# Hybrid attention block on one core: output banks by which branch ended first, and early merges in front of a step's low parts

## Chip, core and metric

One core of a Trainium2 chip runs the whole program. The time is device microseconds of one execution, and lower is better. The engines are TensorE (PE, with its weight loads as PEld), VectorE (DVE), ScalarE (ACT), GpSimd (POOL) and SyncE (SP), which here only issues transfers.

## The reference, cut to what matters

The block normalises a sequence of 1024 tokens, projects it once, and runs two groups of attention heads on the result: a native sparse attention with 8 query heads in 2 groups, and a latent attention with 8 heads. Both are gated, joined, projected back and normalised. The change touches the sparse attention alone. Each of its query tiles of 128 tokens is attended three times:

```python
s_cmp = einsum('bsghd,bngd->bghsn', qg, kc) * scale        # compressed keys (63 of them)
o_cmp = einsum('bghsn,bngd->bsghd', softmax(s_cmp), vc)
s     = einsum('bgqhd,bgqnkd->bgqhnk', qc, kg) * scale     # selected blocks of 64 keys, causal
o_slc = ...                                                # (top 16 of 16 blocks: all causal keys)
s_win = einsum('bnqghd,bnkgd->bnghqk', qw, kband) * scale  # window of 512 keys
o_win = ...
o = g[..., 0:1] * o_cmp + g[..., 1:2] * o_slc + g[..., 2:3] * o_win
```

## The kernel before

**Units, branches, blocks, pairs.** The sparse attention goes over 16 units `u`: query tile `t = u // 2` and head group `g = u % 2`, four heads side by side in 512 columns. A unit has three branches: 1 the window, 2 the compressed keys, 0 the selected blocks. A branch is cut into blocks of 128 keys; the compressed branch is a single block. The list `blocks` names them in order: for each unit the window's blocks with the compressed block put in after the second of them (before the only one of tile 0), and then the selected blocks. Two neighbours of the list make a pair, 74 in all, and pair `i` may end one unit and begin the next. Unit 0 and unit 1 have 3 blocks each, units 2 and 3 have 5, units 4 and 5 have 7.

**A step.** The loop at the end of the listing runs step `i` over the pairs. `scores(i)` are four matmuls and up to two mask matmuls into one of three score buffers in PSUM. `exps(i)` are two exponentials on ACT, one to f32 (`E`) and one to f16 (`H`). `lows(i - 1)` is one DVE subtraction (`L` = `E` - `H`, line 1010). Then come the merges of what ended in the step before, and `weigh(i - 3)`, the 24 small matmuls by which the pair's weights meet the values (line 937). At a branch's last block, `weigh` returns the branch, and the next step merges it: `merge` (lines 953 to 970) takes a reciprocal of the row sums, multiplies by the gate, and scales the 128 x 256 outputs into the tile `mixn` (line 964, the first branch of a unit) or into `tmp` (line 967), which POOL adds to `mixn` (line 968).

**Banks.** The outputs of a branch are summed in one of two PSUM banks, `o0` and `o1`. The window's lie in bank 1, those of the two other branches in bank 0. A bank's next user waits on the chip until the merge of the last one has read it. PE's instructions are in the order in which the program is written, while those of the other engines are put in order ahead of time by a scheduler that takes what is ready, earlier lines first.

**Staging a unit.** `prep(u)` (lines 850 to 860) readies a unit's queries. Two transfers copy 64 rows into `qa`, PE transposes 24 columns of negative row maxima into an output bank (`nmT`, line 855), DVE copies them out (`mr`, line 857), and four transfers put them over the first six rows of the unit's own query tile (line 859). The first score matmul of a block reads `qa` (line 994), the second reads the tile with the new rows (line 995). Units 0 to 3 are staged earlier. `prep_next(u + 3)`, called in each step behind `weigh`, stages the next unit of `todo` when it is no more than three ahead, and only if no window branch is under way in bank 1.

**Side work.** From step 4 on, each step also does one piece of the list `work`: weights of the latent attention are loaded through one buffer named `raw`, and split by ACT and DVE into high and low parts (lines 1050, 1051, 1062, and 1080 for the four loads `wq`). Masks are made by POOL and cast by DVE (line 870).

Of the kernel before, what the change touches and what calls it, by code (L numbers as in the profile page):

```python
# [53 lines left out]
EARLY = 2  # L54
# [6 lines left out]
CMP_AT = (1, 12, 20, 28, 30, 44, 52, 60)  # L61
LAG = 3
SIDE = 4
SIDE_LAT = 36
LATE = 44
E_MIX = 8
# [28 lines left out]
def f32(ap):  # L95
    return ap.bitcast(F32)
# [11 lines left out]
def hybrid_block(ctx, tc, x, c, positions, ada_w, ada_b, norm_g, w_in, cmp_pos, cmp_k_w1, cmp_k_w2,  # L108
# [8 lines left out]
    def pool(stack, name, side="left"):  # L117
        return stack.enter_context(tc.tile_pool(name=name, bufs=1, side=side, reuse_waits="tile"))
# [20 lines left out]
    def o_bank(name, i):  # L139
        return ps_o.tile([P, 512], F32, tag=f"o{i}", name=name, bufs=1)  # L140
# [637 lines left out]
    bm = pool(nsa_s, "bm")  # L778
# [72 lines left out]
    def prep(u, pl, bufs, pn):  # L851
        qa = pl.tile([P, 512], F32R, name=f"qa{u}", tag="qa", bufs=bufs)
        nc.sync.dma_start(f32(qa[:64]), f32(qc[u][:64]))
        nc.sync.dma_start(f32(qa[64:]), f32(qc[u][:64]))
        nc.tensor.transpose(pn[:24, :P], f32(hl24[:, u]), ident)
        mr = pl.tile([24, P], F32, name="mr", tag="mr", bufs=bufs // 2)
        nc.vector.tensor_copy(mr, pn[:24, :P])
        for h in range(4):
            nc.sync.dma_start(f32(qc[u][:6, h * P:(h + 1) * P]), mr[h:24:4])
        staged[u] = qa  # L860
# [74 lines left out]
    def pv(po, c0, ph, pl, n, qs, v, start, stop):  # L935
        for j, (a, lo, hi) in enumerate(((ph, 0, 65), (ph, 65, 129), (pl, 0, 65))):
            nc.tensor.matmul(po[:, c0:c0 + hi - lo], a[:n, qs], v[:, lo:hi], start=start and j == 0, stop=stop and j == 2,  # L937
                             skip_group_check=True)
# [8 lines left out]
    nc.gpsimd.affine_select(emask, emask, pattern=[[-1, P]], compare_op=ALU.is_gt, fill=FAR, base=0, channel_multiplier=1)  # L947
    emr = npool.tile([P, P], F32R, name="emr")
    nc.vector.tensor_copy(emr, emask)
    outs, begun = {}, set()  # L950

    def merge(u, br):
        t, g = divmod(u, G)
        ov = outs.pop(br)[:, :260].rearrange("p (h d) -> p h d", h=4)
        cf = npool.tile([P, 4], F32, name="cf", tag="cf", bufs=4)
        nc.vector.reciprocal(cf, ov[:, :, DH])
        nc.vector.tensor_tensor(cf, cf, gv[:, br, t, g * 4:(g + 1) * 4], op=ALU.mult)
        o, cfb = ov[:, :, :DH], cf[:, :, None].to_broadcast([P, 4, DH])
        if t not in mixes:
            mixes[t] = npool.tile([P, 512], F32, name=f"mixn{t}", tag="mixn", bufs=2)  # L960
        mv = mixes[t][:, g * 256:(g + 1) * 256].rearrange("p (h d) -> p h d", h=4)
        if u not in begun:
            begun.add(u)
            nc.vector.tensor_tensor(mv, o, cfb, op=ALU.mult)  # L964
            return
        tmp = npool.tile([P, 4, DH], F32, name="tmp", tag="tmp", bufs=2)
        nc.vector.tensor_tensor(tmp, o, cfb, op=ALU.mult)  # L967
        nc.gpsimd.tensor_tensor(mv, mv, tmp, op=ALU.add)  # L968
        if br == 0 and g == G - 1:
            nc.sync.dma_start(mix_dram[t * P:(t + 1) * P, :], mixes.pop(t))  # L970

    blocks = []
    for u in range(NT * G):
        t = u // G
        win = [(u, 1, j, j == max(0, t - WIN_T), j == t) for j in range(max(0, t - WIN_T), t + 1)]
        win[min(2, t):min(2, t)] = [(u, 2, 0, True, True)]
        blocks += win + [(u, 0, j, j == 0, j == t) for j in range(t + 1)]
    pairs = [blocks[i:i + 2] for i in range(0, len(blocks), 2)]

    kb_late = npool.tile([P, 2, G, S - KB_CUT * P], F32R, name="kb_late")  # L980

# [4 lines left out]
    def scores(i):  # L986
        pS = ps[0].tile([P, 1024], F32, tag="s", name=f"s{i}", bufs=3)
        for n, (u, br, j, _, _) in enumerate(pairs[i]):
            t, g = divmod(u, G)
            ks = slice(j * P, (j + 1) * P)  # L990
            a, b = (kac[:, g], kbc[:, g]) if br == 2 else (ka[br][g][:, ks], kb_of(j)[:, br, g])
            dst = pS[:, n * 512:(n + 1) * 512]
            mk = cmr[t] if br == 2 else dmr if j == t else emr if br == 1 and j == t - WIN_T else None
            nc.tensor.matmul(dst, a, staged[u], start=True, stop=False)  # L994
            nc.tensor.matmul(dst, b, qc[u], start=False, stop=mk is None)  # L995
            if mk is not None:
                nc.tensor.matmul(dst.rearrange("k (h q) -> k h q", h=4), identr, mk[:, None, :].to_broadcast([P, 4, P]),
                                 start=False, stop=True)
        return pS

    def exps(i, pS):
        Et = npool.tile([P, 1024], F32, name=f"E{i}", tag="E", bufs=EB)
        ph = hlp.tile([P, 1024], F16, name=f"H{i}", tag="H", bufs=HB)
        nc.scalar.activation(Et, pS, AF.Exp, scale=SC_NSA)  # L1004
        nc.scalar.activation(ph, pS, AF.Exp, scale=SC_NSA)  # L1005
        return Et, ph

    def lows(i, Et, ph):
        pl = hlp.tile([P, 1024], F16, name=f"L{i}", tag="L", bufs=HB)
        nc.vector.tensor_tensor(pl, Et, ph, op=ALU.subtract)  # L1010
        return ph, pl

    def weigh(i, ph, pl):
        done = []
        for n, (u, br, j, first, last) in enumerate(pairs[i]):
            g = u % G
            if first:
                outs[br] = o_bank(f"o{u}_{br}", 1 if br == 1 else 0)
            v = vc16[:, g] if br == 2 else v16[:, j, br, g]
            for h in range(4):  # L1020
                pv(outs[br], h * 65, ph, pl, P, slice(n * 512 + h * P, n * 512 + (h + 1) * P), v, first and h == 0, last)
            if last:
                done.append((u, br))
        return done

    next_psum("ps_b")
    todo = list(range(2 * EARLY, NT * G))

    def prep_next(u):
        if todo and todo[0] <= u and 1 not in outs:  # L1030
            prep(todo[0], bm, 2 * EARLY, o_bank(f"nmT{todo[0]}", 1))
            todo.pop(0)

    for u in range(2 * EARLY, 4):
        prep_next(u)
# [86 lines left out]
    def first_part(a):  # L1122
        if a == 0:
            khs.append(key_place("kh1", 0, 0))
        else:
            qhs.append(key_place("qh1", 1, 0))
        kq_second(2 * a)
# [16 lines left out]
    def const_rows(i, tiles, hi):  # L1144
        nc.sync.dma_start(f32(tiles[i][64:hi]), f32(tiles[0][64:hi]))
# [65 lines left out]
    def q_rot_rows(heads, parts=(0, 1)):  # L1211
        for a in parts:
            for h in heads:
                i = h % 4
                nc.sync.dma_start(f32((qhs, qls)[a][h % NSETS][64:96]), f32(qrs[i * 32:(i + 1) * 32, a]))
# [182 lines left out]
    last = [lambda: first_part(0), lambda: const_rows(1, khs, 98), lambda: first_part(1), lambda: q_rot_rows((1,), (0,))]  # L1398
    last2 = peak_leads(1) + [lambda: (peak_split(1), max_rows(1))]
    n_pairs = len(pairs)  # L1400
    s_of, e_of, p_of, m_of = {}, {}, {}, {}
    flow = []
    with tc.manual_schedule(engines={mybir.EngineType.PE}):
        for i in range(n_pairs + LAG + 2):
            if i < n_pairs:
                s_of[i] = scores(i)
                e_of[i] = exps(i, s_of.pop(i))
            if 0 <= i - 1 < n_pairs:
                p_of[i - 1] = lows(i - 1, *e_of.pop(i - 1))
            if n_pairs <= i < n_pairs + LAG:  # L1410
                flow.append((i - n_pairs, *scores_m(i - n_pairs)))
            for u, br in m_of.pop(i - 1, ()):
                merge(u, br)
            if 0 <= i - LAG < n_pairs:
                m_of[i] = weigh(i - LAG, *p_of.pop(i - LAG))
            if i < n_pairs:
                u = pairs[i][-1][0]
                before = len(todo)
                prep_next(u + 3)
                if u % G == 0 and u // G + 1 < NT and u // G + 1 not in cmr:  # L1420
                    next_mask(u // G + 1)
                if i in KB_AT:
                    keys_b(kb_late, KB_CUT * P, S, KB_AT.index(i))
                if i >= SIDE and work:
                    work.pop(0)()
                elif i >= SIDE_LAT and side:
                    if (i - SIDE_LAT) % 2 == 0:
                        side.pop(0)()
                elif i >= LATE and late and (len(late) > 6 or (i - LATE) % 2):
                    late.pop(0)()  # L1430
            if i == LAST_AT:
                for f in last:
                    f()
            if i >= PEAK1 and last2:
                last2.pop(0)()
# [160 lines left out]
```

## Time and profile before

| what | value |
|---|---|
| median of 3 runs | 792.07 us |
| lowest and highest of them | 790.29 and 792.58 us |
| the profiled execution, own time | 788.64 us |
| its span, first to last instruction | 786.9 us |
| PE / DVE / ACT / POOL busy | 94% / 74% / 50% / 29% of the span |
| mean granted clock of TensorE | 0.97 of full speed |

The profiled execution is 3.43 us faster than the median of the runs and 1.74 us longer than its span. The sparse attention lies between 353 and 541 us of the span. Rows of the timeline give the start in us, the duration in us, engine, line, operation, what is written and what it is computed from; brackets at the end hold the idle time just before and the instruction that ended it. Matmuls overlap, so the distance from one start to the next is what a matmul costs.

### The profile page before, as it was taken

Reading aid. Unit: us, or ns where it says so; the run is one execution under the profiler, and the core shown is the slowest. Engines: PE = TensorE matmul, PEld = TensorE weight load, DVE = VectorE, ACT = ScalarE, POOL = GpSimd, SP = SyncE. Lnnn points to the kernel's source line nnn. Section 1 sums busy time; section 2 is a strip of 40 time slices with the busy share of each in tenths; the row PEclk is TensorE's granted clock in tenths of the full one; section 3 lists DMA queues with packets and bytes.
Section 4 is the critical chain, followed back from the end, with each engine's and each line's share of the span. In section 5 each row is a group of like instructions: output and inputs, shape, how many; then the busy total and the mean of one; then the engine's idle time right before and its main releaser. Section 6 shows DMA issues by size and latency. Waiting matters only on the chain.

```text
span 786.9 us, 17257 instructions
## 1 busy us (share of the span) xinstructions
PE 739.3 (94%) x6464; PEld 653.9 (83%) x6464; DVE 583.6 (74%) x1549; ACT 396.3 (50%) x697; POOL 228.0 (29%) x287
## 2 busy tenths in 40 slices
PE   4999999999999999997899999999988989999996
PEld 3988998989999999995677887777877777888885
DVE  3688745587688788888898889987888878654433
ACT  5354534133122331217899977987556566632212
POOL 3334433154231143504443312110200040154322
PEclk9599999999999999999999999999999979999999
DMA  8961423242531121103311123013010140435431
GB/s 307 262 197 49 127 55 108 61 121 80 162 95 48 44 52 47 36 31 97 93 47 44 43 56 82 22 57 80 10 28 16 52 151 29 151 131 185 144 113 54
DMA packets 60513, 70.18 MB, mean 89 GB/s; under 512 B 5957, under 2 KB 46728, under 8 KB 60430
## 3 DMA queue, kind: packets, MB, share of 16 engines
q1 hardware_dynamic: 55646, 64.62, 27.8%
q10 hardware_dynamic: 4784, 4.47, 1.7%
q8 instruction: 51, 0.84, 0.4%
q14 instruction: 32, 0.26, 0.1%
HBM read 48.33 MB, written 11.53 MB: 76 GB/s over the span
## 4 chain that ended last, share of the span: by engine, by line
PE 76%; DVE 9%; issue 4%; ACT 4%; DMA 4%; POOL 2%; SPq 1%; POOLq 0%; DVEq 0%; ACTq 0%
PE pj L589 24%; PE out L1528 11%; PE o L937 5%; PE pm L841 4%; PE s L994 3%; PE s L995 3%; PE kcT L321 2%; PE mo L937 2%; PE hid L642 2%; PE kq L1180 2%; PE ms L1301 2%; DVE L L1010 2%; PE ms L1302 2%; PE ms L1303 2%; PE mm L1256 2%
## 5 line engine op out<-in xcount | busy, mean ns | idle before, releaser
L589 PE MATMUL pj<-whi,hh 128*128 128x288 f32 (+2 forms) x544 | 161.4, 297 | 0.0
L589 PE MATMUL pj<-wlo,hh 128*128 128x288 f32 (+2 forms) x544 | 158.6, 292 | 0.0
L589 PE MATMUL pj<-whi,hl 128*128 128x288 f32 (+2 forms) x544 | 157.6, 290 | 0.0
L589 PEld LDWEIGHTS pj<-wlo,hh 128*128 128x128 f32 x544 | 102.5, 189 | 1.4
L589 PEld LDWEIGHTS pj<-whi,hh 128*128 128x128 f32 x544 | 102.5, 189 | 0.4
L589 PEld LDWEIGHTS pj<-whi,hl 128*128 128x128 f32 x544 | 102.2, 188 | 0.0
L1010 DVE TENSOR_TENSOR L<-E,H 128x1024 f16<-128x1024 f32 x74 | 92.0, 1243 | 13.1 <-ACT H L1005 11.4
L799 DVE CUSTOM_DVE_ANT_0 junk<-pm,maskw 128x256 bf16<-128x256 f32 (+3 forms) x160 | 77.7, 486 | 16.4 <-PE pm L841 4.4
L1004 ACT ACTIVATE E<-s 128x1024 f32<-128x1024 f32 x74 | 76.4, 1032 | 19.8 <-PE s L995 12.2
L937 PEld LDWEIGHTS <-H 128*128 128x128 f16 x1184 | 57.2, 97 | 30.2 <-issue 17.5
L968 POOL TENSOR_TENSOR mixn<-mixn,tmp 128x256 f32<-128x256 f32 x32 | 44.8, 1400 | 108.7 <-DVE tmp L967 101.9
L1005 ACT ACTIVATE H<-s 128x1024 f16<-128x1024 f32 x74 | 76.2, 1030 | 0.0
L841 PE MATMUL pm<-ka,qall 128*128 128x448 f32 (+5 forms) x208 | 67.2, 323 | 0.2 <-DVE mp L796 0.2
L937 PE MATMUL o<-v,H 128*128 128x65 f16 (+1 forms) x1056 | 60.0, 195 | 4.6 <-DVE mixn L964 4.6
L211 POOL TENSOR_TENSOR wlo<-wraw,whi 128x288 fp32r<-128x288 f32 (+2 forms) x64 | 51.7, 832 | 31.6 <-ACT whi L210 29.3
L994 PE MATMUL s<-qa,ka 128*128 128x512 f32 x132 | 57.9, 439 | 2.9 <-ACT H L1005 2.5
L937 PE MATMUL o<-v,L 128*128 128x65 f16 x528 | 56.7, 193 | 0.0
L937 PEld LDWEIGHTS <-L 128*128 128x128 f16 x592 | 55.7, 100 | 0.0
L708 ACT ACTIVATE zt<-pj 128x288 f32<-128x288 f32 (+1 forms) x32 | 12.2, 384 | 74.3 <-PE pj L589 62.6
L1314 ACT ACTIVATE lat<-ms 128x1024 f32<-128x1024 f32 (+2 forms) x40 | 32.6, 815 | 31.1 <-PE ms L1303 14.9
L1316 DVE TENSOR_TENSOR mL<-lat,mH 128x1024 f16<-128x1024 f32 (+2 forms) x40 | 39.0, 988 | 9.7 <-ACT mH L1315 9.5
L995 PE MATMUL s<-qall,kb_early 128*128 128x512 f32 x108 | 43.4, 401 | 0.0
(384 smaller groups left out, 1892.1 us busy)
## 6 DMA issues: line engine op xcount, KB each, us to landing
ad<-in_ada_w_dram SPq DMA_DIRECT2D x32, 256.0 KB
wraw<-in_w_in_dram SPq DMA_DIRECT2D x20, 288.0 KB
x<-in_x_dram SPq DMA_DIRECT2D x8, 512.0 KB
gw<-in_ada_w_dram SPq DMA_DIRECT2D x32, 128.0 KB
qa<-qall SPq DMA_DIRECT2D x32, 128.0 KB
wor<-in_w_out_dram SPq DMA_DIRECT2D x16, 256.0 KB
xr<-in_x_dram SPq DMA_DIRECT2D x8, 512.0 KB
out_dram<-y SPq DMA_DIRECT2D x7, 512.0 KB
```

Of the source, the lines that this page charges most:

```text
L211: split.tensor_tensor(wlo[:, :width], raw[:, j, :width], f32(whi[:, :width]), op=ALU.subtract)
L589: nc.tensor.matmul(pt[:, :width], a[k][:, ts], b[:, :width], start=(n == 0), stop=(n == 23))
L799: nc.vector.tensor_tensor_reduce(out=junk[:, :w], in0=scores, in1=mask, scale=1.0, scalar=2.0 * NEG, op0=ALU.add, op1=ALU.max, accum_out=dst)
L841: nc.tensor.matmul(bank[:, :total_w], lhs, keys, start=True, stop=True)
L937: nc.tensor.matmul(po[:, c0:c0 + hi - lo], a[:n, qs], v[:, lo:hi], start=start and j == 0, stop=stop and j == 2, skip_group_check=True)
L968: nc.gpsimd.tensor_tensor(mv, mv, tmp, op=ALU.add)
L994: nc.tensor.matmul(dst, a, staged[u], start=True, stop=False)
L995: nc.tensor.matmul(dst, b, qc[u], start=False, stop=mk is None)
L1004: nc.scalar.activation(Et, pS, AF.Exp, scale=SC_NSA)
L1005: nc.scalar.activation(ph, pS, AF.Exp, scale=SC_NSA)
L1010: nc.vector.tensor_tensor(pl, Et, ph, op=ALU.subtract)
L1528: nc.tensor.matmul(po, a[:, kk], b[hf][k][:, cs.start - hf * 512:cs.stop - hf * 512], start=(n == 0), stop=(n == 23))
```

## The change

The change has three parts. The first is the order of blocks of units 0 and 1: the compressed block now stands behind the only window block. The second is the choice of banks: a walk over the list gives every branch, at its first block, the bank that is not held and whose last user ended longest ago; and `prep_next` takes either bank, if one holds no branch that is not yet merged, where before it was bank 1 alone. The third is the place of merges in a step: for units below `FIRST_U = 6`, which are the first three query tiles, they are written in front of `lows(i - 1)` and no longer behind it.

```diff
+FIRST_U = 6
-    outs, begun = {}, set()
+    outs, begun, out_bank = {}, set(), {}
...
-        win[min(2, t):min(2, t)] = [(u, 2, 0, True, True)]
+        at = min(2, t) if t else 1
+        win[at:at] = [(u, 2, 0, True, True)]
         blocks += win + [(u, 0, j, j == 0, j == t) for j in range(t + 1)]
     pairs = [blocks[i:i + 2] for i in range(0, len(blocks), 2)]
+    bank_of, ended, held = {}, [-1, -2], {}
+    for n, (u, br, j, first, last) in enumerate(blocks):
+        if first:
+            held[br] = bank_of[u, br] = min((b for b in range(2) if b not in held.values()), key=lambda b: ended[b])
+        if last:
+            ended[held.pop(br)] = n
...
             if first:
-                outs[br] = o_bank(f"o{u}_{br}", 1 if br == 1 else 0)
+                outs[br] = o_bank(f"o{u}_{br}", bank_of[u, br])
+                out_bank[br] = bank_of[u, br]
...
     def prep_next(u):
-        if todo and todo[0] <= u and 1 not in outs:
-            prep(todo[0], bm, 2 * EARLY, o_bank(f"nmT{todo[0]}", 1))
+        free = [b for b in (1, 0) if b not in [out_bank[br] for br in outs]]
+        if todo and todo[0] <= u and free:
+            prep(todo[0], bm, 2 * EARLY, o_bank(f"nmT{todo[0]}", free[0]))
             todo.pop(0)
...
                 e_of[i] = exps(i, s_of.pop(i))
+            for u, br in [m for m in m_of.get(i - 1, ()) if m[0] < FIRST_U]:
+                merge(u, br)
             if 0 <= i - 1 < n_pairs:
                 p_of[i - 1] = lows(i - 1, *e_of.pop(i - 1))
...
-            for u, br in m_of.pop(i - 1, ()):
+            for u, br in [m for m in m_of.pop(i - 1, ()) if m[0] >= FIRST_U]:
                 merge(u, br)
```

## Rows read from the trace of the kernel before

**Rows 1.** The page, busy time of each engine
```profile
PE 739.3 (94%) x6464; PEld 653.9 (83%) x6464; DVE 583.6 (74%) x1549; ACT 396.3 (50%) x697; POOL 228.0 (29%) x287
```

**Rows 2.** By stretch: length; PE, PEld, DVE, ACT, POOL busy; granted clock; DMA
```profile
363.50:370.20 6.70, 3.43 (x30) 2.50 (x27) 6.70 (x19) 3.60 (x6) 4.21 (x3) 0.76 0.39 108
370.20:381.40 11.20, 10.67 (x148) 8.20 (x145) 10.34 (x26) 10.30 (x14) 6.27 (x7) 0.99 0.30 80
381.40:387.50 6.10, 3.73 (x35) 2.92 (x36) 5.88 (x20) 2.89 (x8) 1.64 (x1) 0.72 0.21 55
...
400.00:420.00 20.00, 20.00 (x294) 15.92 (x294) 18.05 (x36) 19.09 (x21) 9.40 (x8) 1.00 0.17 43
```

**Rows 3.** Waits of PE from 353 to 545: total us, times, longest
```profile
PE o L937 <- DVE mixn L964: 4.6, 6, 2.4
PE o L937 <- DVE tmp L967: 3.9, 3, 3.3
```

**Rows 4.** Timeline of PE: long waits, and stretches at either clock
```profile
367.04 0.29 PE L937 MATMUL o<-vc,H 128*128 128x65 f16 x2 [3.27 <-DVE tmp L967]
...
383.77 0.23 PE L937 MATMUL o<-v,H 128*128 128x65 f16 x2 [2.38 <-DVE mixn L964]
...
384.92 0.40 PE L855 MATMUL nmT<-ident,hl 128*24 128x128 f32 x1
...
386.83 0.63 PE L995 MATMUL s<-qall,kb_early 128*128 128x512 f32 x1
387.26 0.31 PE L937 MATMUL o<-v,H 128*128 128x65 f16 x2
...
392.41 0.24 PE L937 MATMUL o<-v,H 128*128 128x65 f16 x2 [0.94 <-DVE mixn L964]
...
393.16 0.27 PE L855 MATMUL nmT<-ident,hl 128*24 128x128 f32 x1
...
394.43 0.23 PE L937 MATMUL o<-v,H 128*128 128x65 f16 x2
...
397.05 0.23 PE L937 MATMUL o<-vc,H 128*128 128x65 f16 x2 [0.32 <-DVE tmp L967]
...
399.44 0.23 PE L937 MATMUL o<-v,H 128*128 128x65 f16 x2 [0.21 <-DVE mixn L964]
```

**Rows 5.** Timeline of DVE around the long waits
```profile
370.75 0.18 DVE L956 RECIPROCAL cf<-o 128x4 f32<-128x4 f32 x1 [0.37 <-PE o L937]
...
380.45 0.96 DVE L1051 TENSOR_TENSOR wnl<-wq,wnh 128x256 fp32r<-128x256 f32 x1
...
381.81 0.24 DVE L956 RECIPROCAL cf<-o 128x4 f32<-128x4 f32 x2
...
382.16 1.22 DVE L1010 TENSOR_TENSOR L<-E,H 128x1024 f16<-128x1024 f32 x1
383.30 0.42 DVE L964 TENSOR_TENSOR mixn<-o,cf 128x256 f32<-128x256 f32 x1
...
386.51 0.27 DVE L857 COPY mr<-nmT 24x128 f32<-24x128 f32 x1
...
389.46 1.23 DVE L1010 TENSOR_TENSOR L<-E,H 128x1024 f16<-128x1024 f32 x1 [2.08 <-ACT H L1005]
```

**Rows 6.** Timeline of SP's queue: start, time of all issues in the row
```profile
375.99 6.25 SPq L1080 DMA_DIRECT2D wq<-in_w_q_up_dram  x2
...
386.99 0.53 SPq L1080 DMA_DIRECT2D wq<-in_w_q_up_dram  x1
387.61 2.91 SPq L859 DMA_DIRECT2D qall<-mr  x4
...
394.75 2.83 SPq L859 DMA_DIRECT2D qall<-mr  x4
```

**Rows 7.** Latent attention: SP's issue of two small transfers, and the matmul that waited
```profile
575.72 1.40 SPq L1281 DMA_DIRECT2D qh<-mrow  x2
...
578.36 0.47 PE L1301 MATMUL ms<-qh,kh 98*128 98x512 f32 x1 [0.25 <-DMA qh<-mrow]
```

## The prediction

> **What bounds the kernel now.** I read the page first: PE is busy for 94% of the span, DVE for 74% [rows 1]. By that the kernel is PE's, and a change that leaves PE's work alone (the same matmuls, three pairs of them in another order) can only act where PE waits. The second view is the table of busy time by stretch. It shows that the start of the sparse attention is another regime: from 363.5 to 370.2 PE is busy for 3.43 of 6.70 us and DVE for all 6.70; from 370.2 to 387.5 DVE is busy for 16.22 of 17.30; from 400 on PE is busy for 20.00 of 20.00 us at full clock [rows 2]. So DVE sets the pace until about step 16, PE after it, and what is won or lost by 400 us goes through to the end one for one. The third view, PE's waits, puts 8.5 us on the merges: 4.6 on `mixn` and 3.9 on `tmp`, with longest waits of 2.4 and 3.3 us [rows 3]. The timeline of PE says where. The 3.27 us before 367.04 are step 4: the second block of pair 1 (unit 1, compressed) wants bank 0, which the first block of the same pair (unit 0, selected) has only just filled. The 2.38 us before 383.77 are step 10: unit 3's selected blocks want bank 0 behind the merge of its compressed block. Three shorter ones of 0.94, 0.32 and 0.21 us follow by 399.44 [rows 4]. The granted clock is 0.76 and 0.72 in the two stretches with the long waits [rows 2].
>
> The clock has a price in rows. From 383.77 the 24 small matmuls of step 10 cost 1.15 us and step 11's scores with the transpose 2.34 us; the same after 392.41, at full clock, cost 0.75 and 1.27 us (steps 13 and 14, with the same 24 small matmuls, and a transpose and five score matmuls) [rows 4]. That is 1.47 us lost behind one long wait.
>
> **Part 1, order and banks.** A walk over the list by hand: unit 0 now has window 1, compressed 0, selected 1; unit 1 window 0, compressed 1, selected 0; from unit 2 on the banks are those of before. So the wait inside step 4 goes: every block now wants a bank that was filled a step earlier. What is late next is the merges themselves, since DVE had no idle time there: with no less DVE work, PE is only released earlier to wait at the next merge. Worth for certain is the time in which DVE itself waited for PE, 0.37 us before 370.75 [rows 5]. At the other end, if DVE were not the limit, it is the whole 3.27 us. I take the lower end, because DVE is the fuller engine in rows 2.
>
> **Part 3, merges in front.** In step 10 DVE did a low part at 382.16 and the merge that PE waited for at 383.30: 1.14 us that now fall behind the merge [rows 5]. Before it stand weight splits from 380.45 to 381.81, 1.36 us of side work [rows 5], written in an earlier step; they pass behind the merge only if the scheduler sees the merge as ready first. Low parts that start 1 us later hurt nobody: they are needed two steps after. With a shorter wait the 24 small matmuls may run at full clock (0.40 us). So the end of step 10, the transpose at 384.92 (call it T), comes 0.37 + 1.14 + 0.40 = 1.9 us earlier without the splits and 3.3 with them; the lowest is 0.37, if DVE's order stays. I take 2.6, the middle of the two: the moved merges pull DVE's whole order towards them in each of steps 4 to 10, so some side work is passed. T is then 382.3.
>
> **Part 2, the staging.** This is where I expect the gain to go. Units 4 to 15 were staged in steps 1, 4, 10, 13, 17, 21, 25, 26, 30, 36, 41, 47. Walking the new rule, they are staged in 1, 10, 11, 13, 17, 18, 21, 24, 29, 36, 41, 47. Their first blocks are in pairs 8, 11, 15, 19, 24, 29, 35 and so on. Unit 5 thus falls from seven steps ahead of use to one: in steps 4 to 9 both banks now hold an unmerged branch at the end of each step, because unit 0's and 1's branches alternate over them. It is staged at the end of step 10, and the second block of step 11's scores is unit 5's. PE's order is fixed, so its matmul on line 995 waits for the whole chain: transpose, copy on DVE, four transfers issued one by one on SP, and the landing. The two `qa` transfers depend on no bank, so I leave them where they were.
>
> The chain's price: unit 6's transposed at 384.92, its last transfer issued by 387.61 + 2.91 = 390.52, which is 5.60 us; unit 7's from 393.16 to 394.75 + 2.83, which is 4.42 us [rows 4, 6]. Landing: two transfers of the same kind ended issue at 577.12 and let a matmul go at 578.36, 1.24 us later [rows 7]. Together 5.66 to 6.84 us; I take 6.3, the middle. Before, that matmul came at 386.83, 1.91 us after T [rows 4]. So it comes 6.3 - 1.9 = 4.4 us later against T than before, with a wait on PE of some 5 us in it. Both long waits of before were followed by a low clock, so I add 1.47 us, less the 0.2 that before still lost behind 386.83 (half of the 0.43 us from there to 387.26): 1.3 us. In return DVE has 5 us to clear its queue, and the waits of 0.94, 0.32 and 0.21 us should go: 1.5 us back. The idle DVE before 389.46 [rows 5] only moves: it waits for step 11's scores as it did before.
>
> The Trainium skill (DMA: Bandwidth & Descriptors, Anatomy of one DMA) gives about 2.0 us as the fixed cost of one DMA on GpSimd's path, most of it the receipt of the write. With that in place of the 1.24 us, the estimate for the chain would be 0.8 us longer and the final time 794.5 us. The trace shows the shorter figure for SP's small transfers, and I keep it.
>
> Other stagings: unit 6 goes from step 10 to 11, four steps ahead of its use; steps cost 2.39 us there (387.26 to 394.43 are three [rows 4]), 9.6 us against a chain of at most 6.84, so it is covered; with another 2.7 us of delay it is not. Units 6, 9, 11 and 12 now use bank 0, so the next `weigh` there waits for the copy on DVE: 1.59 us after the transpose in the one case, (386.51 - 384.92) [rows 4, 5], with 1.27 us of scores as cover; 0 to 0.3 each, 0 to 1.2 in all. Before had the same on bank 1, so I take 0.
>
> **The sum.** -2.6 + 4.4 + 1.3 - 1.5 = +1.6 us. Lowest of the unknowns: -3.3 + 3.75 + 1.3 - 1.5 = +0.3. Highest: -0.4 + 4.9 + 1.3 + 1.2, with no later wait gone, +7.0. On the profiled execution's 788.64 that is 790.2; the median of the runs shown is 792.07, so there it is 793.7.
>
> **Rivals.**
> - DVE is not the limit in steps 4 to 10 (faster). Then both long waits and one loss of clock go before T: 3.27 + 2.38 + 1.47 = 7.1 us, and -7.1 + 4.4 + 1.3 - 1.5 = -2.9, so 789.2. It decides once T comes before about 378. For it: 1.36 us of side work is in front of a merge in rows 5 and more may be. Against it: DVE's full stretches in rows 2. Chance 0.16.
> - SP's queue holds unit 5's rows back (slower). The load `wq` stands at 386.99, right before unit 6's rows; one earlier pair of loads kept the queue for 6.25 us, as the second waited for its buffer [rows 6]. If unit 5's four transfers stand behind that load and it goes no earlier, they start at 387.61 and have landed at 391.76, 4.9 us later than the matmul of before, whatever T was: 4.9 + 1.3 - 1.5 = +4.7, 796.8 us. For it: the order of before. Against it: with earlier merges the splits that free the buffer come earlier. Chance 0.25.
> - The change does not delay unit 5 in effect: its rows land in time, or the wait falls where PE would wait for DVE anyway. Then -2.6 - 1.5 = -4.1, 788.0 us. Against it: PE has about 1 us of matmuls between the transpose and the use, and four issues alone take 2.8. Chance 0.04.
> - My forecast, gain and new wait near to each other: chance 0.55, of which the lower two thirds stay within 2.4 us.
>
> **How the numbers follow.** 0.3% is 2.4 us, about what a measurement of this kernel can tell from no change. Faster: 0.04 and nearly all of 0.16, less what stays under 2.4 us, 0.17. Slower: 0.25 of the queue and some 0.13 of my own case, 0.38. The rest is 0.45. The range reaches from just above the first rival to the queue's price, 790.0 to 797.2; my own case alone has 792.4 to 795.5.
>
> **What would show it.** Right: no wait of PE at line 937 in the second half of step 4; the transpose of unit 5 near 382; behind it a wait of about 5 us at line 995 released by a transfer `qall<-mr`, then a clock near 0.7; no waits on merges from 390 to 400; PE full from 402 on. Wrong: no wait on `mr`'s transfers, or T before 378 (then faster); unit 5's transfers issued after a `wq` load at 387, or a second such wait at unit 6 (then slower).

## The result, and the profile after

| | before | changed |
|---|---|---|
| median (lowest to highest) of 9 runs each | 790.50 us (787.20 to 792.58) | 795.19 us (791.35 to 799.06) |
| ratio, 95% interval | | 1.0073 (1.0048 to 1.0097) |
| profiled execution, its span | 788.64 us, 786.9 us | 795.96 us, 794.1 us |

The change makes the kernel slower by 0.7%. Three single executions of later programs (2427.01, 796.76 and 795.13 us, of the merges alone, the early staging with POOL and all three) count as slow and are left out of the ratios. The time lies in the predicted range, and in the place predicted there is a wait of 4.85 us; but the likeliest sum was +1.6 us, and that is far too small. In the listing after, line 937 has become 938, 964 and 967 are 965 and 968, 994 and 995 are 1002 and 1003, 1005 is 1013, 1010 is 1018, 1051 is 1061, 855, 857 and 859 are 856, 858 and 860, 1080 is 1090; programs made by further edits can differ from these by a few lines.

The page shows the same work on each engine as before, in a longer span [rows 1]:

```profile
PE 737.6 (93%) x6464; PEld 650.1 (82%) x6464; DVE 583.3 (73%) x1549; ACT 395.6 (50%) x697; POOL 226.6 (29%) x287
```

Busy time by stretch (length; PE, PEld, DVE, ACT, POOL busy; granted clock; DMA share, GB/s), to be held against [rows 2]:

```profile
363.50:370.20 6.70, 3.56 (x34) 2.61 (x33) 6.32 (x21) 3.49 (x6) 3.53 (x4) 0.94 0.31 76
370.20:381.40 11.20, 9.70 (x120) 7.33 (x119) 9.29 (x29) 9.50 (x14) 5.31 (x6) 0.88 0.24 64
381.40:387.50 6.10, 1.91 (x29) 1.40 (x29) 4.27 (x11) 1.66 (x5) 2.37 (x2) 0.91 0.28 62
387.50:400.00 12.50, 11.13 (x130) 8.63 (x130) 7.55 (x22) 8.54 (x16) 2.29 (x4) 0.77 0.25 76
400.00:420.00 20.00, 18.96 (x278) 15.06 (x279) 18.38 (x37) 18.84 (x21) 8.48 (x8) 1.00 0.14 37
```

From 381.4 to 387.5 PE works for 1.91 of 6.10 us; the next 12.5 us run at a granted clock of 0.77; and from 400 on there is still 1.04 us of PE idle. The waits of PE from 353 to 545 (total us, times, longest), against [rows 3]:

```profile
PE s L1003 <- DMA qall<-mr: 4.8, 1, 4.8
PE o L938 <- DVE tmp L968: 2.7, 4, 0.9
PE o L938 <- DVE mixn L965: 2.7, 4, 1.3
PE s L1002 <- ACT H L1013: 2.5, 3, 1.3
PE o L938 <- DVE vtop L1078: 2.4, 1, 2.4
```

The three rows of line 938 sum to 7.8 us where before had 8.5: the merges were hardly waited for any less. New is the first row. The timeline of PE, against [rows 4]:

```profile
361.29 0.23 PE L938 MATMUL o<-v,H 128*128 128x65 f16 x2 [0.69 <-DVE mixn L965]
362.76 0.23 PE L938 MATMUL o<-v,H 128*128 128x65 f16 x2 [0.93 <-DVE tmp L968]
365.30 0.24 PE L938 MATMUL o<-vc,H 128*128 128x65 f16 x2 [0.76 <-DVE tmp L968]
368.23 0.24 PE L938 MATMUL o<-v,H 128*128 128x65 f16 x2 [2.38 <-DVE vtop L1078]
...
381.37 0.23 PE L938 MATMUL o<-v,H 128*128 128x65 f16 x2 [1.25 <-DVE mixn L965]
...
382.12 0.27 PE L856 MATMUL nmT<-ident,hl 128*24 128x128 f32 x1
...
388.16 0.77 PE L1003 MATMUL s<-qall,kb_early 128*128 128x512 f32 x1 [4.85 <-DMA qall<-mr]
...
390.07 0.41 PE L856 MATMUL nmT<-ident,hl 128*24 128x128 f32 x1
...
392.41 0.33 PE L938 MATMUL o<-vc,H 128*128 128x65 f16 x2
...
397.75 0.22 PE L938 MATMUL o<-v,H 128*128 128x65 f16 x2 [0.40 <-DVE mr L858]
400.51 0.23 PE L938 MATMUL o<-vc,H 128*128 128x65 f16 x2 [0.81 <-DVE tmp L968]
403.21 0.23 PE L938 MATMUL o<-v,H 128*128 128x65 f16 x2 [0.54 <-DVE mixn L965]
```

Of the 3.27 us inside step 4, 0.93 us are left (362.76); so far part 1 is right. In step 5 stands a new wait of 2.38 us. Unit 5's queries are transposed at 382.12, their matmul goes at 388.16. DVE, against [rows 5], and SP's queue, against [rows 6], show why:

```profile
365.16 1.22 DVE L1018 TENSOR_TENSOR L<-E,H 128x1024 f16<-128x1024 f32 x1
366.29 0.68 DVE L958 TENSOR_TENSOR cf<-cf,gv 128x4 f32<-128x4 f32 x1
...
367.02 0.41 DVE L1061 TENSOR_TENSOR wkl<-wkv,wkh 128x256 fp32r<-128x256 f32 x1
367.36 0.41 DVE L1061 TENSOR_TENSOR wvl<-wkv,wvh 128x256 fp32r<-128x256 f32 x1
...
367.78 0.39 DVE L965 TENSOR_TENSOR mixn<-o,cf 128x256 f32<-128x256 f32 x1
...
380.90 0.42 DVE L965 TENSOR_TENSOR mixn<-o,cf 128x256 f32<-128x256 f32 x1
...
381.56 1.21 DVE L1018 TENSOR_TENSOR L<-E,H 128x1024 f16<-128x1024 f32 x1
...
382.79 0.25 DVE L858 COPY mr<-nmT 24x128 f32<-24x128 f32 x1
```

```profile
383.22 2.90 SPq L860 DMA_DIRECT2D qall<-mr  x4
386.24 0.37 SPq L1090 DMA_DIRECT2D wq<-in_w_q_up_dram  x1
```

The merge that ends the new wait, at 367.78, stands behind a low part, a product and two weight splits. (The row of PE names `vtop`, a side instruction that no matmul reads. I take the merge just before it for the releaser: it ended at 368.17, 0.06 us ahead of the matmul, much as the merge of 380.90 ended 0.05 us ahead of the matmul at 381.37.) In step 10 the merge at 380.90 now is ahead of the low part at 381.56, as predicted. The four rows are issued from 383.22 to 386.12, ahead of the `wq` load at 386.24, so the rival of the SP queue did not happen.

**A finer measure.** Totals of one kernel spread by some 8 us. The traces say where: in the 14 profiled executions of this study the first score matmul comes between 349.45 and 355.27 us, and from the first matmul of the latent attention (`mo`) to the end it takes 242.3 to 246.4 us. The loop between them is what the experiments mostly edit, so I also measure each step by the start of its first score matmul less that of step 0, read from the timelines of PE. The whole loop, to the first `mo`, is 190.92 us before and 196.66 us after, +5.74. (The two profiled spans differ by 7.2: the loop of the second began 1.92 us earlier, and some 3.4 us more went by behind it, a spread that the runs below have too.) Its two ends, before and then after:

```profile
353.60 0.50 PE L994 MATMUL s<-qa,kac 128*128 128x512 f32 x1 [0.46 <-DVE mp L799]
...
544.52 0.26 PE L937 MATMUL mo<-vm,mH 128*128 128x65 f16 x2
```

```profile
351.68 0.50 PE L1002 MATMUL s<-qa,ka 128*128 128x512 f32 x1 [0.46 <-DVE mp L800]
...
548.34 0.26 PE L938 MATMUL mo<-vm,mH 128*128 128x65 f16 x2
```

By steps, difference to before in us (a minus is earlier):

```
step             5      7     10     11     12     13     14     17     23     52
after        -2.69  +0.77  +0.66  -0.91  +3.97  +5.39  +4.31  +5.69  +5.80  +5.76
```

Part 1's gain is there at step 5, 2.69 us, and is given back by step 7. The merge that now stands in front brings 1.57 us between steps 10 and 11. Then come the staging wait, the low clock up to step 13, one us back, and 1.4 us lost again. From step 17 on the distance changes by less than 0.2 us.

Two pairs of programs tell how fine the measure is. The merges alone (below) have the order of instructions of before on all five engines, and still differ from before by up to 0.62 us at a step and by 0.56 us in the loop. The shorter chain (below) is the changed kernel up to the transfers that it moves, and still is 0.87 us behind it at step 10. So a difference of less than 0.9 us between two single traces is not read as an effect here.

### The profile page after: what moved, and what is told of

It is laid out like the page before. It is cut to its first block, busy times and chain, and to the rows that moved or that the text cites. A ratio compares the mean times of both kernels' runs of the same rounds, so it can differ in the third digit from the quotient of the medians.

```text
span 794.1 us, 17260 instructions
## 1 busy us (share of the span) xinstructions
PE 737.6 (93%) x6464; PEld 650.1 (82%) x6464; DVE 583.3 (73%) x1549; ACT 395.6 (50%) x697; POOL 226.6 (29%) x287
## 4 chain that ended last, share of the span: by engine, by line
PE 75%; DVE 9%; DMA 6%; ACT 4%; issue 3%; POOL 1%; SPq 1%; POOLq 0%; DVEq 0%; ACTq 0%
PE pj L590 23%; PE out L1540 11%; PE o L938 6%; PE pm L842 4%; PE s L1002 4%; PE s L1003 3%; PE kcT L322 3%; PE mo L938 2%; PE ms L1311 2%; PE hid L643 2%; PE ms L1312 2%; PE ms L1313 2%; PE mm L1266 1%; PE kq L1190 1%; PE qr L1235 1%
## 5 line engine op out<-in xcount | busy, mean ns | idle before, releaser
L969 POOL TENSOR_TENSOR mixn<-mixn,tmp 128x256 f32<-128x256 f32 x32 | 42.8, 1336 | 109.9 <-DVE tmp L968 103.1
```

## The experiments

**Staging alone.** The order of blocks, the banks and the merges of before; only the steps and banks in which units are staged are those of the changed kernel.

```diff
-    def prep_next(u):
-        if todo and todo[0] <= u and 1 not in outs:
-            prep(todo[0], bm, 2 * EARLY, o_bank(f"nmT{todo[0]}", 1))
+    STAGE = {5: (10, 1), 6: (11, 0), 7: (13, 1), 8: (17, 1), 9: (18, 0), 10: (21, 1), 11: (24, 0), 12: (29, 0),
+             13: (36, 1), 14: (41, 1), 15: (47, 1), 4: (1, 1)}
+
+    def prep_next(i):
+        if todo and i == STAGE[todo[0]][0]:
+            prep(todo[0], bm, 2 * EARLY, o_bank(f"nmT{todo[0]}", STAGE[todo[0]][1]))
...
-                prep_next(u + 3)
+                prep_next(i)
```

> The order of blocks, the banks and the place of merges of before; only the staging steps are those of the changed kernel (unit 5 in step 10, one step ahead of its use, unit 6 in step 11, and so on). Staging theory (the one-step lead of unit 5 is the loss): a wait of 4.5 to 6 us on the transfers of mr before unit 5's first score matmul on line 995, a low clock after it, 4 to 7 us slower than before, ratio 1.005 to 1.009. Banks theory (the new order of units 0 and 1 and what DVE's order makes of it is the loss, and the staging wait only takes the place of a wait on DVE): the wait is there, but the time stays within 2 us of before, ratio 0.998 to 1.003.

795.18 us, ratio 1.0078 (1.0052 to 1.0104), loop +4.64 us.

```profile
380.78 0.24 PE L937 MATMUL o<-v,H 128*128 128x65 f16 x2 [2.39 <-DVE mixn L964]
381.79 0.40 PE L855 MATMUL nmT<-ident,hl 128*24 128x128 f32 x1
...
388.56 0.77 PE L995 MATMUL s<-qall,kb_early 128*128 128x512 f32 x1 [4.66 <-DMA qall<-mr]
```

The old wait of 2.39 us is still in it, and the staging wait of 4.66 us comes on top. Staging alone gives a loss as large as the whole change's.

**The change without the late staging.** Unit 5 is staged in step 2, all else as changed.

```diff
-                prep_next(u + 3)
+                prep_next(u + (4 if i == 2 else 3))
```

> The changed kernel, but unit 5 is staged in step 2, nine steps ahead, while both banks are still empty. Staging theory: no wait on mr's transfers; what is left is the earlier end of step 10 (0.9 us in the changed kernel) and the clock, so 0 to 4 us faster than before, ratio 0.995 to 1.000. Banks theory: still slower than before by 3 us or more, ratio over 1.004.

790.53 us, ratio 1.0008 (0.9986 to 1.0030), loop +0.62 us. No matmul waits for a transfer of `mr`. The price of the earlier staging stands in steps 2 and 3, and is 1.60 us at the start of step 4:

```profile
355.35 0.28 PE L856 MATMUL nmT<-ident,hl 128*24 128x128 f32 x1 [1.34 <-DVE mr L858]
357.48 0.50 PE L1005 MATMUL s<-cm,identr 128*128 128x512 f32 x1 [0.86 <-DVE cm L871]
```

Take the late staging away and the loss is gone, but no gain is left either: with the price of the earlier staging in them, parts 1 and 3 bring nothing measurable here.

**The merges alone.** Before, with part 3 only.

```diff
+            for u, br in [m for m in m_of.get(i - 1, ()) if m[0] < FIRST_U]:
+                merge(u, br)
...
-            for u, br in m_of.pop(i - 1, ()):
+            for u, br in [m for m in m_of.pop(i - 1, ()) if m[0] >= FIRST_U]:
```

> The kernel before with the third part of the change alone: merges of units 0 to 5 written in front of the step's low part. All five engines' instructions stand in the same order as before. If order is all there is: ratio 1.000 within the noise, the low part at the same place in front of the merge that PE waits for in step 10, 2.4 us. If the place in the text acts by itself (the prediction's 1.14 us): the merge comes first, 1 to 3 us faster.

790.18 us, ratio 0.9991 (0.9963 to 1.0020), loop -0.56 us; the waits stand where they stood, 3.27 and 2.41 us long. Laid side by side, the two programs have the same order of instructions on all five engines, and so has the changed kernel with `FIRST_U` at 0 and at 16. Part 3 is a change of the text only: the scheduler puts DVE's work in order by readiness, and where the lines stand decided nothing.

**A shorter chain.** The changed kernel, with two of unit 5's four row transfers issued on ACT.

```diff
-            nc.sync.dma_start(f32(qc[u][:6, h * P:(h + 1) * P]), mr[h:24:4])
+            eng = nc.scalar if u == 5 and h % 2 else nc.sync
+            eng.dma_start(f32(qc[u][:6, h * P:(h + 1) * P]), mr[h:24:4])
```

> The changed kernel with two of unit 5's four row transfers issued from ACT instead of SP, so the four issues take about 1.4 us in place of 2.9. If PE's wait is the chain of the staging, its 4.85 us fall by 1.3 to 1.5 us to about 3.4, and the time by 1 to 2 us against the changed kernel: ratio to before 1.005 to 1.006 where the changed kernel had 1.0073. If the wait is set by something else (the copy of qa, DVE), it stays at 4.6 to 5.

795.61 us, ratio 1.0075 (1.0048 to 1.0102), loop +5.20 us. ACT's rows first, then PE's:

```profile
382.30 1.60 ACTq L861 DMA_DIRECT2D qall<-mr  x1
...
383.94 0.67 ACTq L861 DMA_DIRECT2D qall<-mr  x1
```

```profile
381.24 0.27 PE L856 MATMUL nmT<-ident,hl 128*24 128x128 f32 x1
...
385.92 0.77 PE L1004 MATMUL s<-qall,kb_early 128*128 128x512 f32 x1 [3.50 <-DMA qall<-mr]
```

From transpose to matmul it is 4.68 us instead of 6.04, and the wait is 3.50 us instead of 4.85, as expected. But in this trace the transpose comes 31.32 us after step 0 and not 30.44, though the order up to it is that of the changed kernel, so the loop is only 0.54 us shorter, less than the measure can tell. From the transpose to the first `mo` it is 1.42 us shorter, about the 1.36. The expected gain of 1 to 2 us in the time was not shown.

**Side work later.** Is DVE's side work what keeps the gain of the banks from lasting? Four runs start it in step 12 or in step 24 instead of 4, with the program of before and with the change staged early. The edit of two of them:

```diff
-SIDE = 4
+SIDE = 12
```

> The kernel before with the side work (weights of the latent attention) begun in step 12 instead of step 4, so that DVE is spared about 5 us of splits and sums in steps 4 to 10. If DVE's load sets the pace there: from the first score matmul of the sparse attention, step 10 ends 3 to 5 us earlier than the 31.3 us of before, the 2.4 us wait in step 10 falls under 1 us, the wait inside step 4 to 1.5 to 2.5 us, and the time falls by 2 to 5 us, ratio 0.994 to 0.998. If the waits are set by the chain between the engines and not by load: step 10 ends within 1 us of before, ratio 0.999 to 1.001.

> The changed kernel with unit 5 staged in step 2 and the side work begun in step 12. If the banks do take away the wait inside step 4 and only DVE's load gave it back in step 5 (2.4 us), that wait now falls under 1 us, and the kernel beats the kernel before by more than side work alone does: 4 to 7 us, ratio 0.991 to 0.995. If the new banks are worth nothing by themselves: the same as side work alone, 0.994 to 0.998.

> The same with the side work begun in step 24, where a unit has more blocks and so fewer merges in a step. By the load theory the same gain as with step 12 or up to 2 us more, as the work no longer meets the merges of units 4 to 6; by the other theory no difference to step 12.

> The kernel before with the side work begun in step 24. By the load theory 2 to 5 us faster than before, and slower by 1 to 3 us than the changed banks with unit 5 staged early and the same side work, which is what the banks alone are worth; if the banks are worth nothing, the two are within 1 us.

| | time, us | ratio (95%) | step 7 | step 16 | step 23 | step 41 | loop |
|---|---|---|---|---|---|---|---|
| before, 12 | 789.90 | 1.0007 (0.9980 to 1.0034) | +0.89 | -1.50 | +0.25 | +0.20 | +0.28 |
| early, 12 | 788.56 | 1.0005 (0.9979 to 1.0031) | -0.68 | -1.16 | +0.94 | +1.00 | +1.03 |
| early, 24 | 790.71 | 1.0022 (0.9993 to 1.0051) | -1.67 | -3.21 | -3.33 | -1.69 | -1.71 |
| before, 24 | 793.43 | 1.0062 (1.0031 to 1.0093) | +0.76 | -2.00 | -1.86 | +1.35 | +1.39 |

No time fell, where the load theory had every one of them fall by 2 us or more, and the last is slower, clear of noise. The edit also spared DVE less than its constant says: with 24 and the old banks, DVE is busy for 27.52 us from 353 to 387.5 where before has 30.11, since the scheduler still put the splits of the first two loads there. Only the four `wq` loads moved out. The end of step 10, which was to come 3 to 5 us earlier if DVE's load sets the pace there, came 0.45 us later, 0.68 later, 1.15 earlier and 0.38 later, in the order of the table. Yet later steps show what the times hide. With 24, step 16 comes 2.00 us earlier with the old banks and 3.21 us with the new ones. Between steps 28 and 41, where the work was put, the old banks lose all of it and more, the new ones about half. There ACT and PE have no room: PE is busy for 5.00 and ACT for all 5.00 us from 440 to 445 in the kernel before. The two programs with 24 differ by the change and the early staging alone: the new banks are ahead by 3.10 us in the loop and by 2.7 us in the medians, with intervals of the ratios that still overlap.

**The splits' subtractions on POOL.** This does spare DVE. Three programs: before, the change staged early, and the change.

```diff
-        nc.vector.tensor_tensor(lo, src, f32(hi), op=ALU.subtract)
+        nc.gpsimd.tensor_tensor(lo, src, f32(hi), op=ALU.subtract)
```

> The kernel before, with the subtraction of the weight splits of the side work moved from DVE to POOL; PE's instructions and their order stay. This takes off DVE, from step 4 to step 11, four pairs of splits, some 4 us of the 30.11 us that it is busy from 353 to 387.5. Theory A (DVE's load sets the pace of steps 4 to 10): the transpose of step 10 comes 1.5 to 4 us earlier after the first score matmul than the 31.32 us of before, and the time falls by 1.5 to 4 us (786.5 to 789 where the kernel before has 790.5). Theory B (the pace is set by the way from a merge to the next matmul, each a wait on two or three engines in turn, and not by DVE's sum of work): the transpose moves by less than 1 us and the time stays within 1.5 us, 789 to 792. Theory C (POOL, which adds the branches and now has the splits in front of its additions, takes DVE's place): later, 792 to 795.

> The changed kernel with unit 5 staged in step 2 and the splits on POOL: new banks, no staging wait, DVE relieved by some 4 us before step 11. Theory A: the banks are worth something once DVE has room, so this is faster than the kernel before by 3 to 6 us (784.5 to 787.5), and faster than the kernel before with the splits on POOL. Theory B: the same as the kernel before within 1.5 us, 789 to 792. Theory C: slower, 792 to 795.

> The changed kernel as it is, with the splits on POOL. The chain from the transpose of unit 5 to its matmul has no split in it, so both theories expect the staging wait to stay at 4 to 5.5 us. Theory A: the transpose comes 1.5 to 4 us earlier and the time falls to 791 to 794. Theory B: time as the changed kernel's, 794 to 797.

| | time, us | ratio (95%) | step 5 | step 8 | step 12 | step 16 | step 19 | loop |
|---|---|---|---|---|---|---|---|---|
| before | 791.13 | 1.0015 (0.9989 to 1.0041) | +0.30 | +1.53 | -2.25 | -2.36 | +1.09 | +1.23 |
| early | 789.02 | 0.9997 (0.9968 to 1.0026) | -3.08 | +1.34 | -1.41 | -1.39 | +0.75 | +0.62 |
| changed | 799.21 | 1.0113 (1.0071 to 1.0155) | -2.05 | +1.87 | +4.05 | +5.50 | +5.98 | +5.85 |

The first two are ahead by 2.25 and 1.41 us at step 12 and lose it by step 19. In the first of them, ACT and then PE:

```profile
391.10 0.42 ACT L1050 ACTIVATE wnh<-wq 128x256 fp32r<-128x256 f32 x1 [2.17 <-DMA wq<-in_w_q_up_dram]
```

```profile
395.89 0.24 PE L937 MATMUL o<-v,H 128*128 128x65 f16 x2 [2.16 <-DVE mixn L964]
```

ACT waits 2.17 us for a load, with the exponentials of the next step behind it in its order; DVE's next low part waits 2.35 us for those, and PE 2.16 us for the merge that DVE does behind it. `raw` is one buffer: this load was issued at 388.57, as POOL ended the last subtraction of the load before (386.89 + 1.66 us). POOL's splits of 128x256 took 0.73 to 1.71 us there, DVE's 0.41 to 0.96. There, what DVE no longer holds up, the buffer does, through ACT. The second has such a wait of ACT too (1.41 us), and a wait of PE of 1.42 us for a copy `mr` in step 18, where it loses most of its lead. In the changed kernel the staging wait is still 4.61 us, as expected. Its time, of six executions, lies above both expectations and some 3 to 4 us above the changed kernel's, though its loop is only 0.11 us longer: by the traces, what is added lies outside the loop.

**All three.** Early staging, side work from step 24, subtractions on POOL.

> The changed kernel with unit 5 staged in step 2, the side work from step 24 on, and the splits' subtractions on POOL. By the starts of the steps, the kernel with the late side work alone was 3.3 us ahead of the kernel before at step 23 and lost 1.6 of it again from step 28 to 39, where PE waited for a branch merge on DVE, DVE and ACT both being some 95% busy there. If DVE is what the late side work loads (A), the lead at step 23 stays and the loss of 1.6 falls below 0.6, since 4 us of subtractions leave DVE: the loop is 2.7 to 3.5 us shorter than before's, the time 785 to 788. If it is ACT, whose half of the splits stays (B), the loss stays at 1.2 to 2 us and the time at 787 to 791. If POOL's additions become late behind the splits (C), the loop loses more than 2 us after step 23.

791.95 us, ratio 1.0024 (0.9991 to 1.0057), loop -0.40 us: above every time that was expected. The lead is 3.62 us at step 23 and still 3.26 at step 37; at step 41 it is 0.38. ACT in between:

```profile
437.54 0.42 ACT L1060 ACTIVATE wnh<-wq 128x256 fp32r<-128x256 f32 x1 [1.41 <-DMA wq<-in_w_q_up_dram]
```

Theory A falls: 3.24 us are lost after step 23, though DVE was relieved. ACT has a part in it (B): it waits for the load and then works without a break to 451 us, with the exponentials late. PE's own waits there are 0.80 us for those exponentials, and 0.68 and 0.91 us for DVE. By size it is C: without POOL the same steps 37 to 41 lost 0.82 us, with it 2.88, and it is POOL that frees `raw`. How much falls to each was not separated.

No version here is shown to be faster than the kernel before. Shortest in the loop is the early staging with side work from step 24, by 1.71 us, but its time is not lower. By the middle of their ratios, the three kernels with side work from step 24 are 1.7, 4.9 and 1.9 us slower, with loops of -1.71, +1.39 and -0.40 us: some 2 to 3.5 us seem to be lost outside the loop. The traces show a place where such a difference lies, 86 to 117 us behind the first `mo`. There before has one stretch of low clock, and the changed kernel two (before first, then the changed kernel):

```profile
630.50:644.50 14.00, 11.71 (x106) 10.45 (x105) 10.29 (x16) 8.23 (x12) 6.21 (x5) 0.63 0.47 160
644.50:661.50 17.00, 15.40 (x179) 13.03 (x176) 15.32 (x36) 11.60 (x18) 1.26 (x1) 1.00 0.09 33
```

```profile
634.30:648.30 14.00, 9.77 (x112) 8.54 (x111) 9.23 (x14) 8.04 (x13) 6.82 (x5) 0.88 0.48 160
648.30:665.30 17.00, 15.89 (x123) 12.52 (x124) 13.52 (x30) 9.72 (x15) 1.85 (x2) 0.70 0.11 33
```

Ten of the 14 traces have two such stretches, all three with side work from step 24 among them, and take 244.4 to 246.4 us from the first `mo` to the end; the four with one take 242.3 to 242.9. Whether a kernel has the second one in every execution is not shown, as there is one trace of each.

## Why the prediction was right and wrong

That the time lies in the range owes something to luck. The range was built on 792.07 us, the median of three runs; nine runs give 790.50. Its upper end is 5.1 us above its own base, and the change cost 4.7 us by the medians and 5.8 us by the ratio. The likeliest outcome named, no change within 0.3% (0.45), did not come; slower had 0.38.

The four terms of its sum, measured on the steps (T is the transpose in step 10):

| term | predicted | changed | staging alone |
|---|---|---|---|
| T, after step 0 | -2.6 | -0.88 | -0.11 |
| T to unit 5's matmul, less 1.91 | +4.4 | +4.13 | +4.86 |
| from there to step 13 (low clock) | +1.3 | +2.14 | +1.14 |
| from step 13 to the end | -1.5 | +0.35 | -1.25 |
| sum | +1.6 | +5.74 | +4.64 |

**The staging: right.** Unit 5 is staged at the end of step 10 and used in step 11; the wait is 4.85 us where "some 5 us" were forecast, 6.04 us from transpose to matmul where 6.3 were taken, at the line and with the releaser named. With the late staging alone the loss is all there, and without it all gone. The rival that says the change does not delay unit 5 falls, and so does the SP queue [rows 6]: the `wq` load that was to stand ahead of the rows came 0.12 us behind the last of them.

**The landing.** From the end of the last issue to the matmul it is 2.04 us in the changed kernel, and 1.17 us with the staging alone (issued until 387.39), 1.31 us with two queues and 1.16 us with the splits on POOL. The 1.24 us of [rows 7] was the better guess in three of four. The Trainium skill (DMA: Bandwidth & Descriptors, Anatomy of one DMA) has about 2.0 us fixed for one DMA on GpSimd's path; on SP's queue, the changed kernel's trace comes to the same size, and the other three are below it. About half a us of the difference can be seen in the DMA packets of the traces: in the changed kernel five of the six packets of the last row start from 386.77 to 386.83, and the sixth at 387.31, as an 8 KB packet of the kind `instruction` (386.79 to 387.31) ends. In the other three programs the six start within 0.07 us. In ten of the other 13 traces, too, a late packet of such a row starts within 0.02 us of the end of a packet of that kind. What makes the rest was not tried.

**T, the step that failed first.** Two things were wrong in the -2.6. The splits that were to be passed by the moved merges were not passed, since part 3 moves nothing; the low part behind the merge in step 10, which did come, belongs to the new times of the plan and not to the lines' place. And part 1 did not bring 0.37 us for certain and then nothing: it brought 2.69 us by step 5, and the next merge in DVE's order, behind 1.22 + 0.68 + 0.75 us of other work, took it back with a wait of 2.38 us. The text said that PE "is only released earlier to wait at the next merge"; this is what happened: +0.66 us at step 10, and the merge in front makes it -0.91 at step 11. So T came 0.88 us earlier after step 0 where 2.6 were forecast, and 0.01 us earlier in the shorter chain, whose order up to T is the same: its gain is not clear of nothing. That it stands at 382.12, as forecast for 382.3, is chance, as the loop began 1.92 us earlier.

**The later waits, the step that failed most.** The waits from 392 to 400 were to go, as DVE has 5 us to clear its queue. With the old banks that is right: staging alone has -1.25 us there. With the new ones 0.40, 0.81 and 0.54 us stand in steps 14 to 17 instead, 1.75 us in place of 1.47 [rows 4]. None is for a unit staged through bank 0; the copy waited for at 397.75 is unit 7's, in bank 1 as before. What differs is ACT's wait for the `wq` load. In the changed kernel and with the staging alone:

```profile
396.12 0.42 ACT L1060 ACTIVATE wnh<-wq 128x256 fp32r<-128x256 f32 x1 [1.54 <-DMA wq<-in_w_q_up_dram]
```

```profile
386.38 0.42 ACT L1053 ACTIVATE wnh<-wq 128x256 fp32r<-128x256 f32 x1 [4.23 <-DMA wq<-in_w_q_up_dram]
```

With the staging alone it lies inside the staging wait, where ACT has nothing else to do; in the changed kernel one comes later, ahead of the steps that lose. The two other programs with the new banks and the late staging have it late too, 1.88 us (the shorter chain) and 1.58 us (subtractions on POOL), and get nothing back behind step 13 either (+1.15 and +0.16 us). That it makes the three waits was not tried.

**The clock.** Priced from one long wait of before, 1.3 us; it came to 2.14. Behind 388.16 the 24 small matmuls take 1.34 us (1.15 behind the long wait of before) and the transpose with five score matmuls 2.34 (390.07 to 392.41), as before; but the low clock goes on into the next step, to about 393.3:

```profile
386.40:393.30 6.90, 5.14 (x48) 4.06 (x48) 2.45 (x7) 3.38 (x7) 0.27 (x2) 0.51 0.31 90
```

**DVE as the limit.** The rival "DVE is not the limit" would need T before about 378; T is at 382.12, and the 2.69 us at step 5 did not last. With less of DVE's work in front, step 16 comes 1.2 to 3.2 us earlier in all six such programs. But the end of step 10, the place of the rival, moved by no more than 1.15 us either way, so what relief of DVE is worth in steps 4 to 10 is not shown. That it does not shorten the kernel is shown. That this is because ACT and PE are full where the work goes fits the late losses, and was not separated from the buffer. With side work late, the new banks are worth 1.47 us at step 23 (-3.33 against -1.86) and 3.10 us at the end of the loop; with it in place and unit 5 staged early, nothing that can be told (+0.70 against 0 at step 23).

## What to carry to other kernels

A rule that gives a scarce buffer to whoever asks first also decides when the buffer is *empty*: look for the one who only gets in when nobody holds it, here the staging of the next unit, and walk the list for its slack. A wait on a merge that is removed is worth what the next merge lets through, so walk on to the next one before a gain is booked. And where totals spread by more than the effect, the start of each step in the trace, less that of the first, shows where time is won and where it is given back, once two traces of the same order of instructions have shown how far it can be trusted (here 0.9 us).

## What was not expected of the hardware

The loop is far steadier than the kernel: from step 42 on the steps of all these programs keep their distance to before within 0.1 us. The spread of the totals is mostly outside it: 5.8 us in the start of the loop, 4.1 us behind it. Both go with TensorE's granted clock. In the first 60 us it is at half for 13.7 to 17.1 us in the seven traces whose loop begins at 349.45 to 351.68, and for 20.5 to 27.3 us in the seven that begin at 353.55 to 355.27; behind the loop it is the second stretch of low clock shown above. Whether the clock makes the delay or goes with it was not tried. And the landing of the same small transfers differs by 0.9 us from one program to another; about half a us of that is one packet that starts only as a packet of the kind `instruction` ends.
